# Triangular inverses in a gated-delta-net layer: two row groups' 32x32 products issued alternately, and the third set of products issued at once

## The chip, the cores and the metric

The kernel runs on one core of one Trainium2 chip. The time is that of one execution on the device, in microseconds (us), of the slowest core, which here is the only one. Matrix products run on TensorE (PE in the profile), the loads of their stationary operands are counted apart (PEld), and the other engines are VectorE (DVE), ScalarE (ACT), GpSimd (POOL) and SyncE (SP), which here only issues DMAs.

## The reference, cut to what matters

Two layers on x of 1024 tokens by 1024 features in float32: layer 0 is chunked softmax attention, layer 1 is gated DeltaNet, and each is followed by a dense squared-ReLU MLP. The change lies in layer 1, in the triangular solve of each of its 8 heads:

```python
L = jnp.where(strict, jnp.einsum('bhnid,bhnjd->bhnij', kb, k) * decay, 0.0)
M = L + jnp.eye(CHUNK, dtype=jnp.float32)
rhs = jnp.concatenate([vb, kb * jnp.exp(gc)[..., None]], axis=-1)
sol = lax.linalg.triangular_solve(M, rhs, left_side=True, lower=True, unit_diagonal=True)
u, w = sol[..., :dv], sol[..., dv:]
```

What follows is a scan over the chunks of a head, which multiplies the solution by the state that the chunks before have left.

## The kernel before, in words

Dense products are made of three matmuls each: weights and activations are split into a high and a low part (`whi`, `wlo`, `xs`), and the three larger of the four products are added up in a PSUM bank of 128x512. These are the rows `acc<-xs,whi` and `acc<-xs,wlo` of the profile, and also `zz<-xs,...` at first.

The DeltaNet layer (`deltanet`, L1700, `dn_run`, L1844) runs 34 panels of dense products (k, q, v and z of 8 heads, and the first two of the output projection), 24 matmuls for each half of a panel. After each single dense matmul it calls `turn` (L1753): every side task that is due gets to issue one step, up to its next `yield`. The side tasks are generators: the blocks of L (`dn_blocks`), the inverses (`dn_inverses`, L2379), the preparation of keys, queries and values, two interleaved scans (`dn_scans`, L2488) and the heads' outputs (`dn_outs`). So the order of the instructions on every engine is fixed when the program is written out. What decides it is a planner's clock (`Clock`, L91), with a price for each instruction: a dense matmul counts 512/2400 us, and a float32 product 32 columns wide counts 32/600 us. A task that has issued a step is due again when the planner takes that step for finished (`t.ready = c.end`), 0.3 us after its last matmul if it ended on TensorE. A task can also wait for another's mark (`until`), for a buffer (`take`) or for a planned time (`sleep`). On the chip each engine then takes its own instructions in that order, held up by semaphores alone. All instructions that are issued under the planner carry the line of its wrapper, L162, so that in the profile they are told apart by tiles.

The kernel takes chunks of 128 tokens, 8 for each head, and inverts each 128x128 triangle by blocks. The four 32x32 blocks on the diagonal are inverted on VectorE in `dn_solves` (L2221), for four heads together; through DRAM they come into `Z` (the tile `Zh`) and, transposed, into `X`. `dn_inverse` (L2290), once for each head, puts in the rest:

- Step 1 (L2319 to L2327): for the two 64x64 triangles of a chunk (e = 0 and 1), the block beside the diagonal (`U12`, tile `ua`) times `X`. These are 8 products of 32x32 (one for each chunk p) for each e. A product with e = 0 reads partitions 0 to 31 and writes 32 to 63; one with e = 1 reads 64 to 95 and writes 96 to 127. In the profile they are `tp<-X,ua`. VectorE then scales both results into `ua` (L2330, `ua<-tp,nbr`).
- Step 2 (L2333 to L2340): these times the inverted diagonal blocks of `Z`, again 8 products for each e, here reading partitions 32 to 63 or 96 to 127 (`tp<-Zh,ua`).
- After a `yield`, 8 further products for e = 0 alone with the operands exchanged (L2341 to L2343, `tp<-ua,Zh`), into the same PSUM tile `tp`; I call these the third group. After another `yield` ScalarE copies all of it out (L2345 to L2348, `X<-tp` and `Zh<-tp`).
- Two further steps of 64x64 products (`tp<-X,ub` and `tp<-Zh,ub`) complete the inverse.

A float32 product stands in the trace as two passes, each a weight load and a matmul, so 16 products are 32 rows of the trace. All products of a step go into one PSUM bank (`tp`, taken in turn from two). Before the change the 8 products with e = 0 come first and then the 8 with e = 1.

Of the kernel before, what the change touches and what calls it, by code (L numbers as in the profile page):

```python
# [39 lines left out]
def wide(col, p, n):  # L40

    return col.rearrange("p (q o) -> p q o", o=1).broadcast_to([p, col.shape[-1], n])
# [191 lines left out]
class Trunk:  # L234
# [2055 lines left out]
    def dn_inverse(self, h):  # L2290

        nc, db = self.nc, self.db
        Z = self.Zh[h % 3]
        X = self.X[:, :, 0:32]
        U12 = self.dq.tile([P, 8, 32], F32, name=self.nm("ua"), tag="ua")
        U34 = self.dq.tile([P, 8, 64], F32, name=self.nm("ub"), tag="ub")
        for e in range(2):
            nc.sync.dma_start(U12[64 * e : 64 * e + 32], self.u12[h, e])
        nc.sync.dma_start(U34[0:64], self.u34[h])
        nbr = self.sm.tile([P, 8], F32, name=self.nm("nbr"), tag="nbr")  # L2300
        nc.vector.scalar_tensor_tensor(nbr, self.rk[:, h], -1.0, self.cols[:, 1, h], ALU.mult, ALU.mult)
        yield from self.sleep(G["sl_u12"])
        for e in range(2):
            r = slice(64 * e, 64 * e + 32)
            nc.gpsimd.tensor_tensor(U12[r], U12[r], wide(self.rk[r, h], 32, 32), ALU.mult)
        nc.gpsimd.tensor_tensor(U34[0:64], U34[0:64], wide(self.rk[0:64, h], 64, 64), ALU.mult)
        yield from self.until("solve", h // 4)
        if h >= 3:
            yield from self.until("scan", h - 3)
        zd, xd = self.solved[h // 4]  # L2310
        for b in range(4):
            r = slice(b * 32 + (h % 4) * 8, b * 32 + (h % 4) * 8 + 8)
            s = slice(32 * b, 32 * b + 32)
            nc.sync.dma_start(Z[s, :, s], zd[r].rearrange("p c i -> c p i"))
            if b < 3:
                nc.sync.dma_start(self.X[s, :, 32 * (b % 2) : 32 * (b % 2) + 32], xd[r].rearrange("p c i -> c p i"))
        yield from self.sleep(G["sl_inv"] if h % 4 == 0 else G["sl_inv2"])
        yield
        tp = yield from self.take("tp")  # L2319
        ps = tp[:, :256].rearrange("p (q t) -> p q t", t=32)  # L2320
        hT = U12
        for e in range(2):
            r, o = slice(64 * e, 64 * e + 32), slice(64 * e + 32, 64 * e + 64)
            for p in range(8):
                nc.tensor.matmul(ps[o, p], U12[r, p], X[r, p], start=True, stop=True,
                                 tile_position=(64 * e, 64 * e + 32))
        yield  # L2327
        for e in range(2):
            o = slice(64 * e + 32, 64 * e + 64)
            nc.vector.tensor_tensor(hT[o], ps[o], wide(nbr[o], 32, 32), ALU.mult)  # L2330
        self.give("tp", tp)
        yield
        tp = yield from self.take("tp")  # L2333
        ps = tp[:, :256].rearrange("p (q t) -> p q t", t=32)
        for e in range(2):
            r, o = slice(64 * e, 64 * e + 32), slice(64 * e + 32, 64 * e + 64)
            for p in range(8):
                nc.tensor.matmul(ps[r, p], hT[o, p], Z[o, p, o], start=True, stop=True,
                                 tile_position=(64 * e + 32, 64 * e))
        yield  # L2340
        o = slice(32, 64)  # L2341
        for p in range(8):
            nc.tensor.matmul(ps[o, p], Z[o, p, o], hT[o, p], start=True, stop=True, tile_position=(32, 32))  # L2343
        yield
        nc.scalar.activation(self.X[o, :, 0:32], ps[o], AF.Copy)  # L2345
        for e in range(2):
            r, o = slice(64 * e, 64 * e + 32), slice(64 * e + 32, 64 * e + 64)
            nc.scalar.activation(Z[r, :, o], ps[r], AF.Copy)  # L2348
        self.give("tp", tp)
        yield  # L2350
        tp = yield from self.take("tp")
        ps = tp.rearrange("p (q t) -> p q t", t=64)
        r, o = slice(0, 64), slice(64, 128)
        for p in range(8):
            nc.tensor.matmul(ps[o, p], U34[r, p], self.X[r, p], start=True, stop=True, tile_position=(0, 64))
        yield
        nc.vector.tensor_tensor(U34[o], ps[o], wide(nbr[o], 64, 64), ALU.mult)
        self.give("tp", tp)
        yield
        tp = yield from self.take("tp")  # L2360
        ps = tp.rearrange("p (q t) -> p q t", t=64)
        for p in range(8):
            nc.tensor.matmul(ps[r, p], U34[o, p], Z[o, p, o], start=True, stop=True, tile_position=(64, 0))
        yield
        nc.scalar.activation(Z[r, :, o], ps[r], AF.Copy)
        self.give("tp", tp)
        yield
# [351 lines left out]
```

## Time and profile before

| | |
|---|---|
| median of the runs | 2487.07 us |
| the three runs | 2490.65, 2485.62, 2487.07 us |
| time of the profiled execution | 2484.63 us |
| its span, first to last instruction | 2482.9 us |
| mean granted TensorE clock | 0.995 |
| DVE, ACT, POOL busy, share of the span | 72%, 47%, 50% |
| the inverses' steps lie between | 1390 and 1635 us of the span |

The span leaves out 1.7 us of the profiled execution. Busy time of matmuls counts from a row's start to its modelled end, so the rows of a pipelined sequence overlap; how fast such a sequence runs is read from the starts of its rows.

### The profile page before, as it was taken

What the parts mean: (1) busy time and instruction counts of PE and PEld (TensorE: products, weight loads), DVE (VectorE), ACT (ScalarE), POOL (GpSimd) and SP (SyncE); (2) the same over time, 40 slices, a digit from 0 to 9 for tenths busy, and PEclk for the clock granted to TensorE, in tenths of its full rate; (3) what the DMA queues carried; (4) which work ended last, traced back from release to release, by engine and by line L of the source; (5) the groups of instructions that cost most, each with busy time, mean ns of one, the idle gap of its engine ahead of it and who ended that gap; (6) DMA issues with size and microseconds to landing.
All of it is one profiled execution on the core that took longest, in us unless ns stands there. A gap on an engine that the chain in (4) does not pass through costs nothing.

```text
span 2482.9 us, 36204 instructions
## 1 busy us (share of the span) xinstructions
PE 2417.5 (97%) x12556; PEld 2014.5 (81%) x12556; DVE 1789.9 (72%) x3152; ACT 1168.9 (47%) x2209; POOL 1250.5 (50%) x1059
## 2 busy tenths in 40 slices
PE   8999999999999999999999999999999999999997
PEld 6888888777788887887787888888787888888886
DVE  6666656678877678888778776665678777688887
ACT  6666666635455433333463443343345555433333
POOL 2444445623766656666444443433316666476655
PEclk9999999999999999999999999999999999999998
DMA  4222232522555796763265322322415555967842
GB/s 163 70 67 67 73 84 91 185 88 102 216 212 208 277 335 215 255 211 116 97 194 180 93 85 90 92 75 81 182 60 201 201 216 214 354 233 238 257 163 85
DMA packets 199927, 398.92 MB, mean 161 GB/s; under 512 B 53232, under 2 KB 67888, under 8 KB 199744
## 3 DMA queue, kind: packets, MB, share of 16 engines
q1 hardware_dynamic: 180016, 351.50, 42.3%
q10 hardware_dynamic: 19728, 45.12, 4.8%
q8 instruction: 99, 1.62, 0.3%
q14 instruction: 84, 0.69, 0.1%
HBM read 257.43 MB, written 130.71 MB: 156 GB/s over the span
## 4 chain that ended last, share of the span: by engine, by line
PE 70%; DVE 6%; DMA 2%; issue 1%; ACT 1%; POOL 0%; ACTq 0%; DVEq 0%; POOLq 0%; SPq 0%
PE y L1039 26%; PE z L1039 12%; PE acc L162 12%; PE acc L1039 7%; PE tp L162 4%; PE zz L162 2%; PE acc L303 2%; PE acc L305 2%; PE acc L304 2%; PE sb L162 2%; DVE x L1544 1%; DMA wraw<-in_w_up_dram 1%; DVE xs L420 0%; DMA xd<-x 0%; DMA qk<-grows 0%
## 5 line engine op out<-in xcount | busy, mean ns | idle before, releaser
L162 PE MATMUL acc<-xs,whi 128*128 128x512 f32 x1728 | 597.6, 409 | 4.1 <-POOL whi L1043 1.0
L162 PEld LDWEIGHTS acc<-xs,whi 128*128 128x128 f32 x1728 | 315.8, 189 | 53.0 <-POOL whi L1043 1.4
L162 PE MATMUL acc<-xs,wlo 128*128 128x512 f32 x856 | 348.4, 407 | 0.0
L1039 PE MATMUL y<-xs,whi 128*128 128x512 f32 x1008 | 311.6, 390 | 5.2 <-DVE x L1544 1.8
L162 POOL TENSOR_TENSOR wlo<-wraw,whi 128x512 fp32r<-128x512 f32 x126 | 165.4, 1314 | 224.2 <-ACT whi L162 190.6
L1054 POOL TENSOR_TENSOR s<-wraw 128x256 f32<-128x256 f32 (+1 forms) x93 | 90.1, 969 | 358.6 <-DVE a L1045 172.1
L1045 DVE TENSOR_TENSOR wlo<-wraw,whi 128x512 fp32r<-128x512 f32 (+1 forms) x182 | 209.4, 1151 | 25.6 <-ACT whi L1048 25.6
L1039 PEld LDWEIGHTS y<-xs,whi 128*128 128x128 f32 x1008 | 188.9, 188 | 47.1 <-DVE x L1544 2.6
L1048 ACT ACTIVATE whi<-wraw 128x512 fp32r<-128x512 f32 (+2 forms) x191 | 146.4, 766 | 121.7 <-PE y L1039 83.0
L1048 ACT ACTIVATE a<-s 128x256 fp32r<-128x256 f32 x122 | 63.8, 524 | 281.7 <-PE y L1039 141.3
L1039 PE MATMUL y<-xs,wlo 128*128 128x512 f32 x504 | 196.4, 390 | 0.0
L1039 PE MATMUL y<-xs,a 128*128 128x512 f32 x732 | 187.9, 392 | 6.5 <-DVE x L1544 6.5
L1544 DVE TENSOR_TENSOR x<-y,x 128x512 f32<-128x512 f32 x240 | 165.0, 687 | 35.1 <-PE y L1039 28.3
L162 PEld LDWEIGHTS acc<-xs,wlo 128*128 128x128 f32 x856 | 162.4, 190 | 23.2
L1039 PEld LDWEIGHTS y<-xs,a 128*128 128x128 f32 x732 | 136.1, 188 | 40.1 <-DVE x L1544 10.3
L1039 PE MATMUL y<-xs,ahi 128*128 128x512 f32 x512 | 158.9, 391 | 7.8 <-ACT nt L1233 7.8
L1039 PE MATMUL acc<-xs,whi 128*128 128x512 f32 x528 | 162.9, 390 | 0.0
L162 POOL TENSOR_SCALAR pr<-pr,rs 128x640 f32<-128x640 f32 (+4 forms) x128 | 88.6, 696 | 129.0 <-DVE rs L162 99.9
L1039 PE MATMUL z<-xs,whi 128*128 128x512 f32 x480 | 147.8, 389 | 0.0
L1121 DVE TENSOR_TENSOR c<-c 128x512 fp32r<-128x512 f32 x112 | 119.9, 1077 | 30.8 <-POOL c L1051 27.3
L162 DVE CUSTOM_DVE_ANT_0 pr<-sp,bias 128x640 f32<-128x640 f32 (+4 forms) x128 | 83.8, 655 | 63.9 <-PE sp L162 62.9
L162 POOL TENSOR_TENSOR cy<-cy,cz 128x512 f32<-128x512 f32 x48 | 62.7, 1306 | 126.9 <-DVE cz L162 95.8
(370 smaller groups left out, 6047.8 us busy)
## 6 DMA issues: line engine op xcount, KB each, us to landing
xs<-gt SPq DMA_DIRECT2D x256, 256.0 KB, 4.9
gt<-c SPq DMA_DIRECT2D x112, 512.0 KB, 3.0
wraw<-in_w_up_dram SPq DMA_DIRECT2D x64, 512.0 KB, 3.7
wraw<-in_w_down_dram SPq DMA_DIRECT2D x64, 512.0 KB, 4.6
r<-gr SPq DMA_DIRECT2D x88, 256.0 KB, 3.5
wraw<-in_w_in_dram SPq DMA_DIRECT2D x32, 512.0 KB, 3.5
gr<-ssum ACTq DMA_DIRECT2D x62, 256.0 KB, 3.2
wraw<-in_w_qkv_dram SPq DMA_DIRECT2D x30, 512.0 KB, 3.3
```

The lines of the kernel that those rows point to most:

```text
L162: return call(*args, **more)
L303: nc.tensor.matmul(ps, hi[:, k], xh, start=(k == 0), stop=False)
L304: nc.tensor.matmul(ps, hi[:, k], xl, start=False, stop=False)
L305: nc.tensor.matmul(ps, lo[:, k], xh, start=False, stop=(k == KT - 1))
L1039: nc.tensor.matmul(ps, w[:, k], x, start=bool(first and f), stop=bool(last and e), skip_group_check=True)
L1045: self.nc.vector.tensor_tensor(lo, src, hi.bitcast(F32), ALU.subtract)
L1048: self.nc.scalar.activation(hi, src, AF.Copy)
L1054: self.nc.gpsimd.tensor_tensor(out, x, y, ALU.add)
L1121: nc.vector.tensor_tensor(t[z][:, HB:].bitcast(F32R), t[z][:, HB:], t[z][:, :HB], ALU.subtract)
L1544: nc.vector.tensor_tensor(x, ps, x, ALU.add)
```

## The change

In steps 1 and 2 the two loops are exchanged: for each chunk p the product with e = 0 and then that with e = 1 are issued, so that the two row groups alternate one by one. The `yield` between step 2 and the third group is taken out, so that the third group's 8 products follow at once, in the same turn of the planner. Number, operands and places of the products stay.

```diff
-        for e in range(2):
-            r, o = slice(64 * e, 64 * e + 32), slice(64 * e + 32, 64 * e + 64)
-            for p in range(8):
+        for p in range(8):
+            for e in range(2):
+                r, o = slice(64 * e, 64 * e + 32), slice(64 * e + 32, 64 * e + 64)
                 nc.tensor.matmul(ps[o, p], U12[r, p], X[r, p], start=True, stop=True,
                                  tile_position=(64 * e, 64 * e + 32))
         yield
...
-        for e in range(2):
-            r, o = slice(64 * e, 64 * e + 32), slice(64 * e + 32, 64 * e + 64)
-            for p in range(8):
+        for p in range(8):
+            for e in range(2):
+                r, o = slice(64 * e, 64 * e + 32), slice(64 * e + 32, 64 * e + 64)
                 nc.tensor.matmul(ps[r, p], hT[o, p], Z[o, p, o], start=True, stop=True,
                                  tile_position=(64 * e + 32, 64 * e))
-        yield
         o = slice(32, 64)
         for p in range(8):
             nc.tensor.matmul(ps[o, p], Z[o, p, o], hT[o, p], start=True, stop=True, tile_position=(32, 32))
```

## The prediction

> **What bounds the kernel now.** I read the page first, then busy times by stretch, then TensorE's waits around the inverses.
>
> ```profile
> span 2482.9 us, 36204 instructions
> PE 2417.5 (97%) x12556; PEld 2014.5 (81%) x12556; DVE 1789.9 (72%) x3152; ACT 1168.9 (47%) x2209; POOL 1250.5 (50%) x1059
> ```
>
> The busy times by stretch (columns: PE, PEld, DVE, ACT, POOL, the granted clock, DMA):
>
> ```profile
> 1340.00:1640.00 300.00, 298.51 (x2346) 252.94 (x2345) 208.53 (x497) 118.88 (x272) 119.46 (x94) 1.00 0.30 90
> 1640.00:1740.00 100.00, 100.00 (x574) 85.30 (x573) 53.32 (x131) 38.31 (x89) 35.44 (x26) 1.00 0.27 85
> 1740.00:1760.00 20.00, 15.37 (x64) 11.27 (x64) 14.35 (x26) 8.79 (x18) 10.24 (x7) 0.91 0.67 232
> ```
>
> TensorE is busy 298.51 of the 300 us that hold the inverses, and all of the next 100. DVE, the next busiest, has 91 us free in the first stretch. The waits of TensorE between 1385 and 1760 us say the same from the other side:
>
> ```profile
> PE tp L162 <- DVE o L162: 2.9, 1, 2.9
> PE tp L162 <- POOL dc L162: 1.3, 1, 1.3
> PE acc L162 <- ACT xs L162: 0.8, 1, 0.8
> PE sb L162 <- ACT vn L162: 0.4, 1, 0.4
> ```
>
> One wait of 1.3 us belongs to the inverses' stretch; most of the rest is the stage's end. So in this stage a microsecond less on TensorE is nearly a microsecond less of time, unless the new order makes an instruction wait where none did. Whether the inverses are themselves waited for is read from the products that use them:
>
> ```profile
> L162 PE MATMUL zz<-vb,Zh x12: 270/272/275, 1465.0 to 1713.5; 128*128 128x128 f32 x12
> L162 PE MATMUL sb<-vb,Zh x4: 272/274/275, 1405.1 to 1488.9; 128*128 128x128 f32 x4
> L162 ACT ACTIVATE Zh<-tp x24: 373/375/593, 1396.2 to 1634.1; 32x256 f32<-32x256 f32 x16, 64x512 f32<-64x512 f32 x8
> ```
>
> A head's scan begins with its `vb,Zh` product. The last inverse is copied out at 1634.1 us, and the last scan begins 79 us later. An earlier inverse alone therefore brings little. What counts is time on TensorE.
>
> **What step 1 and step 2 cost now.** The matmuls of head 0 from step 1's end to the third group, then one step of head 0, both steps of head 1 and step 2 of head 7 (start, length from the first start to the last end, count):
>
> ```profile
> 1391.87 0.62 PE L162 MATMUL acc<-xs,whi 128*128 128x512 f32 x2
> 1392.33 0.40 PE L162 MATMUL acc<-xs,wlo 128*128 128x512 f32 x1
> 1392.57 0.62 PE L162 MATMUL acc<-xs,whi 128*128 128x512 f32 x2
> 1393.03 0.40 PE L162 MATMUL acc<-xs,wlo 128*128 128x512 f32 x1
> 1393.35 1.09 PE L162 MATMUL tp<-Zh,ua 32*32 32x32 f32 x32
> 1394.38 0.74 PE L162 MATMUL acc<-xs,whi 128*128 128x512 f32 x2
> 1395.05 0.69 PE L162 MATMUL tp<-ua,Zh 32*32 32x32 f32 x16
> 1395.67 0.50 PE L162 MATMUL acc<-xs,wlo 128*128 128x512 f32 x1
> ...
> 1390.35 1.25 PE L162 MATMUL tp<-X,ua 32*32 32x32 f32 x32
> ...
> 1412.47 1.09 PE L162 MATMUL tp<-X,ua 32*32 32x32 f32 x32
> ...
> 1415.53 1.09 PE L162 MATMUL tp<-Zh,ua 32*32 32x32 f32 x32
> 1416.55 0.66 PE L162 MATMUL tp<-ident,qT 128*128 128x128 f32 x4
> ...
> 1418.51 0.69 PE L162 MATMUL tp<-ua,Zh 32*32 32x32 f32 x16
> ...
> 1625.79 1.09 PE L162 MATMUL tp<-Zh,ua 32*32 32x32 f32 x32
> ```
>
> ```profile
> L162 PE MATMUL tp<-Zh,ua x256: 191/191/212, 1393.4 to 1626.7; 32*32 32x32 f32 x128
> ```
>
> One pass lasts 0.19 us, but they are pipelined: 16 passes of one row group take 0.69 us, so 0.50 from the first start to the last, 0.50/15 = 0.033 us apart. Two groups one after the other would take 0.69 + 16 x 0.032 = 1.20 us. They take 1.09. The missing 0.11 lies where the one group gives way to the other, as a count of the passes in step 2 of head 0 shows. Each row begins at 1393.35, and the number in brackets is how many passes have started by its end:
>
> ```profile
> 1393.35:1393.65 0.30, 0.30 (x9) 1.00 1.14 135
> 1393.35:1393.75 0.40, 0.40 (x12) 1.00 1.00 135
> 1393.35:1393.85 0.50, 0.50 (x18) 1.00 0.93 134
> 1393.35:1393.95 0.60, 0.60 (x22) 1.00 0.92 139
> 1393.35:1394.05 0.70, 0.70 (x25) 1.00 0.97 148
> 1393.35:1394.15 0.80, 0.80 (x28) 1.00 0.92 145
> ```
>
> Three passes start in a tenth of a microsecond everywhere, but six between .75 and .85. There the second group already runs while the first's last passes do: TensorE works on both row groups at a time, each at its own pace. It does so only for the few passes that it looks ahead.
>
> **What alternation takes away.** If neighbours in the order always belong to different groups, that overlap holds throughout, and 32 passes take the 0.69 us of one group plus the second's later start. That start is between 0 and one product (two passes, 0.06 us) behind; I take 0.02, hence 0.71 us. The saving is 1.09 - 0.71 = 0.38 us a step. The bounds are 0.40 (no lag) and -0.11 (none of even today's overlap). Of the 16 steps I take 15: head 0's first step takes 1.25 us today, without visible overlap, and the rows do not say what its second group waited for, so I put its saving at zero. 15 x 0.38 = **5.7 us**.
>
> The Trainium skill speaks against this in "TensorE: Matmul & The Clock Gate" (Wait — 56ns, not 53.3ns?): start-to-start never drops below about 25 ns however few the columns are. By that figure a step of 32 passes would come to about 0.97 us by my estimate, and this term to 1.8 us. The trace disagrees at one place, where six starts in 0.1 us are 17 ns apart; no row here shows it for a whole step.
>
> **What the missing `yield` takes away.** Around a step of small products TensorE loses time. Dense matmuls start 0.23 us apart (three from 1392.33 to 1393.03). From step 2's last start (1393.35 + 1.09 - 0.19 = 1394.25) to the third group's first (1395.05) pass 0.80 us with only two dense matmuls in them. Those two cost 0.46 elsewhere, and one step from pass to pass is 0.03, so 0.31 us is paid for leaving the small products and coming back. With the third group directly behind step 2 this is paid once less in each head, whatever stood between (two dense matmuls in head 0, transposes and scan products among others in head 1): 8 x 0.31 = **2.5 us**. From below I bound this by 0, if the two groups' tile positions make the same break; from above by 0.31 + 0.11, if the third group also overlaps the end of step 2's second row group as the groups do now.
>
> **What moves.** The third group issues 8 matmuls and no DMA. It passes what the planner had put between: 2.1 us of work in head 1 (from 1415.53 + 0.90 to 1418.51), 0.8 in head 0. That work starts about 0.5 us later, scan products and transposes among it, and the ACT copies behind the third group come earlier. Behind a late scan product stand a DVE step and the next products of that scan, and their cover is the dense matmuls between; without it a scan step would cost up to its 0.5 us, at most 8 x 0.5 = 4 us. In the alternating order the second product of a step needs the second group's operands, which came 8 products later before. An operand that is late holds the step up no longer than now, since the step's end waited for it anyway. But all 16 products, and the dense ones behind, then stand in line. For step 2 these operands are DVE's scaled results:
>
> ```profile
> 1391.64 0.88 DVE L162 TENSOR_TENSOR ua<-tp,nbr 32x256 f32<-32x256 f32 x2 [0.80 <-PE tp L162]
> ```
>
> In head 0 both are done at 1392.52, 0.83 us before step 2 begins. I cost both effects at nothing and keep the 4 us for the range. From the first head on, the planner may also place later steps of all tasks otherwise, on every queue, SP's and POOL's included. The trace cannot show that, and it is the largest unknown.
>
> **The sum.** 5.7 + 2.5 = 8.2 us off the profiled execution's 2484.63 us gives 2476.4. That execution lay 2.4 us below the median of the three runs; off the median, 2487.07, it gives **2478.9 us**, or 2479.
>
> **The rivals.**
>
> *The overlap does not hold for a whole step.* Both groups write one PSUM bank, and one meeting of three or four passes is all the trace shows. A pace limit midway between the two that the rows show (17 and 33 ns, so 25) would leave a step at 31 x 0.025 + 0.19 = 0.97 us, so 15 x 0.12 + 2.5 = 4.3 us in all: 2482.8. With passes strictly one after the other (1.20 us), the steps lose 15 x 0.11 = 1.7 us, and 2487.07 - 2.5 + 1.7 = 2486.3 is left. For it: the passes at the meeting may have been queued beforehand. Against it: six starts in 0.1 us is exactly double the pace, with both groups in one bank. The Trainium skill states the rule for the strict case in "TensorEngine Tiling (Array Packing)" (Gotcha 1: PSUM Pressure): different row tiles cannot use the same PSUM bank at the same time. By that rule the trace would have no such meeting, and it has one.
>
> *Changing the row group costs something each time.* This is the rival on the slower side. Today each step changes the group once, afterwards 15 times: 14 x 2 x 8 = 224 changes more. At the price of entering a group of small products from dense ones (1393.03 to 1393.35 is 0.32 us, less 0.23, so 0.09), that is 20.2 us, and with today's overlap lost too the time is 2487.07 - 2.5 + 1.7 + 20.2 = 2506.5. It is slower than before from (2.5 - 1.7)/224 = 0.004 us a change. Against it: the one change that a step has now costs less than nothing.
>
> *The gain is eaten by new waits.* TensorE gets ahead, and the chain through the last head's normalization, which it awaits 2.9 us at the stage's end, or that through POOL (1.3 us) does not follow. If half is lost, 2483; if all, 2487. With another idle stretch like the last one, whose window has a clock of 0.91, so 0.09 x 20 = 1.8 us, it is 2489. For it: the order of all later work may shift. Against it: the scans interleave with dense matmuls, and TensorE's four longest waits of the stage add up to 5.4 us. The same shift can gain, too: without these waits and the slow clock (2.9 + 1.3 + 1.8 = 6.0) the time is 2473.
>
> **How the numbers follow.** About 0.2% (5 us) is what a measurement of this kernel can tell from no change, so faster means below 2482.1. I give the forecast 0.60, the incomplete overlap 0.15 (0.09 for the pace limit, 0.06 for strict order), a price per change 0.04 and the eaten gain 0.21. Of the forecast's cases some 0.05 end above 2482.1 by small new waits; of the eaten gain 0.03 stay below. That makes faster 0.58. Slower takes the 0.04 and some 0.05 of the eaten gain whose waits exceed what was won by 5 us: 0.09. The rest, 0.33, is no change. The range goes from 2473, with the stage's own waits gone as well, to 2489, which takes in the incomplete overlap and most of the eaten gain.
>
> **What would show it.** In the changed profile the 32-pass rows, or the count of starts, tell the first term: about 0.7 us a step and six starts in 0.1 us throughout if right; 0.97 or 1.2 if a rival holds. The third group must follow step 2 with no dense matmul between, 48 passes in one stretch of about 1.2 us, and 8 entries less. TensorE's waits between 1385 and 1760 us must stay near these 5.4 us. I am wrong if the steps shrink as said and the time does not: then the waits have grown, and the one that did is named there.

## The result

The changed kernel takes 2478.56 us in the median (2475.62 to 2479.61, 7 runs), the kernel before, timed beside it, 2485.62 us (2481.44 to 2490.65, 7 runs). The ratio is 0.9971 with a 95% interval of 0.9961 to 0.9981: faster by 0.19 to 0.39%, or about 7 us. A second timing on another occasion (below, the last experiment) gave 0.9974 (0.9963 to 0.9984). The forecast was 2479.

The profiled execution after took 2476.15 us. Its page begins:

```profile
span 2474.4 us, 36203 instructions
PE 2406.7 (97%) x12556; PEld 2006.3 (81%) x12556; DVE 1785.7 (72%) x3152; ACT 1169.3 (47%) x2209; POOL 1248.1 (50%) x1059
```

TensorE has as many matmuls as before and is busy 10.8 us less. The span is 8.5 us shorter, but not all of that is the change. The first step 1 began at 1390.35 us before. After, it begins here:

```profile
1387.51 0.24 PE L162 MATMUL tp<-X,ua 32*32 32x32 f32 x2
1388.01 0.69 PE L162 MATMUL tp<-X,ua 32*32 32x32 f32 x30 [0.25 <-DMA X<-xd]
...
1750.71 0.39 PE L303 MATMUL acc<-xs,whi 128*128 128x512 f32 x1
```

Up to that point both programs issue the same instructions in the same order, so 2.84 us of the difference is variation between two executions. (The changed kernel, profiled once more in the last experiment, began this step at 1391.19 us.) What the change does lies behind it. The second row names what head 0's first step waits for here, the landing of `X`, 0.25 us. The last row quoted is the first matmul outside the planned stage. In the profile before, that matmul is

```profile
1759.33 0.39 PE L303 MATMUL acc<-xs,whi 128*128 128x512 f32 x1
```

From the first step 1 to there, the stage took 1759.33 - 1390.35 = 368.98 us before and 1750.71 - 1387.51 = 363.20 us after: 5.8 us less. I use this stage length below, since it leaves out what varied ahead of the change.

**The steps.** Head 1 after (the rows of both steps and the third group; start, length, count):

```profile
1410.19 0.69 PE L162 MATMUL tp<-X,ua 32*32 32x32 f32 x32
...
1412.86 0.60 PE L162 MATMUL tp<-Zh,ua 32*32 32x32 f32 x26
1413.27 0.21 PE L162 MATMUL tp<-ua,Zh 32*32 32x32 f32 x1
...
1413.39 0.57 PE L162 MATMUL tp<-ua,Zh 32*32 32x32 f32 x13
1413.89 0.66 PE L162 MATMUL tp<-ident,qT 128*128 128x128 f32 x4
```

Step 1 takes 0.69 us, as long as one row group alone. How many of its passes have started by the end of each window (the number in brackets):

```profile
1410.18:1410.28 0.10, 0.09 (x6) 1.00 0.02 0
1410.18:1410.48 0.30, 0.29 (x18) 1.00 0.01 0
1410.18:1410.68 0.50, 0.49 (x30) 1.00 0.01 0
```

Six start in each tenth of a microsecond, from the first pass to the last. Step 2 and the third group are one stretch of 48 passes without a dense matmul, 1.10 us from 1412.86 to 1413.39 + 0.57. The third group's first pass starts while six passes of step 2 are still to come.

**The waits.** TensorE's between 1385 and 1755 us after:

```profile
PE tp L162 <- DVE o L162: 2.8, 1, 2.8
PE tp L162 <- DVE vb L162: 1.6, 1, 1.6
PE tp L162 <- DVE kd L162: 1.4, 1, 1.4
PE zz L162 <- DVE st L162: 1.0, 1, 1.0
PE acc L162 <- ACT xs L162: 0.8, 1, 0.8
```

The wait for POOL of 1.3 us is gone, and three waits for DVE of 1.0 to 1.6 us, 4.0 in all, have come. With the smaller rows the list adds up to 8.9 us against 6.0 before.

**The clock.** The windows at the stage's end, before, after, and in a second profile of the changed kernel (the number behind POOL's is the granted clock):

```profile
1725.00:1759.33 34.33, 29.70 (x146) 23.48 (x145) 23.43 (x48) 14.71 (x32) 13.62 (x10) 0.95 0.52 174
```

```profile
1716.00:1750.71 34.71, 30.23 (x149) 23.98 (x148) 23.45 (x49) 14.70 (x32) 13.95 (x10) 0.90 0.51 172
```

```profile
1720.03:1754.74 34.71, 30.08 (x149) 23.89 (x148) 23.56 (x49) 14.70 (x32) 14.03 (x10) 0.95 0.52 172
```

In the first profile after, the clock withheld 0.10 x 34.7 = 3.5 us instead of 0.05 x 34.3 = 1.7. That is a difference between executions and not the change's doing: the second profile of the same kernel has 0.95 like the kernel before. Nor did it lengthen the stage, which takes 363.55 us in the second profile and 363.20 in the first.

### The profile page after: what moved, and what is told of

It is laid out like the page before. It is cut to its first block, busy times and chain, and to the rows that moved or that the text cites. A ratio compares the mean times of both kernels' runs of the same rounds, so it can differ in the third digit from the quotient of the medians.

```text
span 2474.4 us, 36203 instructions
## 1 busy us (share of the span) xinstructions
PE 2406.7 (97%) x12556; PEld 2006.3 (81%) x12556; DVE 1785.7 (72%) x3152; ACT 1169.3 (47%) x2209; POOL 1248.1 (50%) x1059
## 4 chain that ended last, share of the span: by engine, by line
PE 70%; DVE 5%; DMA 2%; issue 1%; ACT 1%; POOL 0%; SPq 0%; ACTq 0%; DVEq 0%; POOLq 0%
PE y L1039 27%; PE z L1039 13%; PE acc L162 11%; PE acc L1039 7%; PE tp L162 3%; PE zz L162 2%; PE acc L303 2%; PE acc L305 2%; PE acc L304 2%; PE sb L162 1%; DVE x L1544 1%; DMA wraw<-in_w_in_dram 1%; DMA wraw<-in_w_up_dram 1%; DVE xs L420 0%; DMA xd<-x 0%
```

## The experiments

The theory: the gain is time on TensorE, from both parts, less what the planner's new order loses. The first rival: the new order itself made the gain, and TensorE's own time mattered little. It can be told apart, because exchanging the loops leaves the planner's prices and with them the order of everything else as it was; only the missing `yield` changes that order. The traces bear this out: apart from the inverses' own products, TensorE, VectorE, ScalarE and GpSimd go through the same sequence of instructions in the kernel before and with the loops alone exchanged, and again in the changed kernel and with the `yield` alone taken out. In each experiment the ratio is to the kernel before, run on the same chip. The stage lengths, read as above in each trace, stand in a table at the end.

### Alternation alone

```diff
 (before, with the loops over p and e exchanged in steps 1 and 2)
                 nc.tensor.matmul(ps[r, p], hT[o, p], Z[o, p, o], start=True, stop=True,
                                  tile_position=(64 * e + 32, 64 * e))
         yield
```

> The row groups alternate in steps 1 and 2, the yield before the third group stays; every engine's order but that of the 32x32 products is the one of before. If the gain is TensorE time: steps of 32 passes in 0.69 us instead of 1.09, 15 x 0.40 = 6.0 us less, ratio to before about 0.9976, and the long waits of TensorE are those of before (2.9, 1.3, 0.8 us). Rival, that the planner's new order made the gain: ratio 1.000, since this order is the old one.

Measured: 2478.01 us, ratio 0.9975 (0.9965 to 0.9985). Head 1, and the wait that the changed kernel no longer has:

```profile
1411.67 0.69 PE L162 MATMUL tp<-X,ua 32*32 32x32 f32 x32
1414.33 0.69 PE L162 MATMUL tp<-Zh,ua 32*32 32x32 f32 x32
...
1416.91 0.69 PE L162 MATMUL tp<-ua,Zh 32*32 32x32 f32 x16
```

```profile
PE tp L162 <- POOL dc L162: 1.3, 1, 1.3
```

In the old order the alternation alone gives 0.25%, as expected from the steps. The rival is refuted: with the order unchanged there should have been nothing. The stage is 4.8 us shorter where the steps give 6.0. Of the rest, 0.8 us are longer waits (6.8 us in all against 6.0), most of it in one place, behind this row of DVE:

```profile
1598.25 2.27 DVE L162 TENSOR_SCALAR ry<-rt 128x8 int32<-128x8 int32 x1
...
1600.83 0.49 PE L162 MATMUL zz<-r,Zh 128*128 128x128 f32 x2 [0.64 <-DVE r L162]
```

In the kernel before the same `ry<-rt` takes 2.28 us, and TensorE, which reaches this point later, does not wait. What makes the row so long is the subject of the experiment with VectorE.

### The third group at once, alone

```diff
 (before)
                 nc.tensor.matmul(ps[r, p], hT[o, p], Z[o, p, o], start=True, stop=True,
                                  tile_position=(64 * e + 32, 64 * e))
-        yield
         o = slice(32, 64)
```

> The old loops (first all products of one row group, then of the other), but the third group follows at once; the order of all other instructions is that of the changed kernel. If the gain is TensorE time: 0.31 us of leaving and coming back and 0.10 of overlap at the third group's start, 8 x 0.41 = 3.3 us less, and the new order's longer waits give back about 2.7 us: ratio 0.9986 to 1.000. Rival, that the new order made the gain: ratio 0.997 as for the whole change.

Measured: 2481.91 us, ratio 0.9991 (0.9982 to 0.9999). Step 2 and the third group of head 1, and the waits:

```profile
1416.04 1.00 PE L162 MATMUL tp<-Zh,ua 32*32 32x32 f32 x29
...
1416.97 0.57 PE L162 MATMUL tp<-ua,Zh 32*32 32x32 f32 x13
```

```profile
PE tp L162 <- DVE vb L162: 1.6, 1, 1.6
PE tp L162 <- DVE kd L162: 1.0, 1, 1.0
PE zz L162 <- DVE st L162: 1.0, 1, 1.0
```

The 48 passes take 1.50 us (1416.04 to 1416.97 + 0.57), 0.10 less than 1.09 and 16 further passes 0.032 us apart. So the third group overlaps the end of step 2 here too. The three new waits are here, with the old loops: they come from the order. They give back most of what this part wins (the waits add up to 8.4 us against 6.0); it is worth about 0.1% by itself, and the stage is only 0.3 us shorter. The first rival asked for 0.997 here and is refuted a second time. On top of alternation the missing `yield` shortens the stage by 0.6 to 1.0 us (364.15 against 363.55 and 363.20), which the times do not resolve: 0.9975 against 0.9974 and 0.9971.

### Row groups changing after every four products

```diff
 (before, in both steps)
-        for e in range(2):
+        for b in range(4):
+            e = b % 2
             r, o = slice(64 * e, 64 * e + 32), slice(64 * e + 32, 64 * e + 64)
-            for p in range(8):
+            for p in range(4 * (b // 2), 4 * (b // 2) + 4):
```

> As before, yield kept, but the row groups change after every four products (e = 0, 1, 0, 1) instead of after eight: three meetings in a step instead of one. If TensorE looks only some three passes ahead, each meeting wins 0.10 us: 32 passes in 1.20 - 0.30 = 0.90 us (first start to last end). Rival, that it overlaps whatever stands in its queue: 0.7 us, as when they alternate one by one. Rival, that a meeting's overlap needs the queue filled beforehand: 1.09 us as before.

Measured in a single execution (2480.44 us, too few to compare times):

```profile
1409.89 0.89 PE L162 MATMUL tp<-X,ua 32*32 32x32 f32 x32
1412.75 0.89 PE L162 MATMUL tp<-Zh,ua 32*32 32x32 f32 x32
```

0.89 us, where 0.90 was expected from three meetings at 0.10 each. So TensorE does not overlap all 32 passes of a step, although they stand in line together. The rows fit a reach of about three passes (0.10 us at 0.032 a pass) at each meeting; that TensorE looks so far ahead is inferred from these lengths. It is why alternation one by one matters. The stage, 367.45 us, is 1.5 us shorter than before and not the 15 x 0.20 = 3.0 that the steps give. Matched instruction by instruction with the kernel before, it is 1.9 us ahead up to 1545 us of that kernel's span and loses 1.1 in the next 4 us, where the clock fell in this execution and not in that one.

### Three groups alternating

```diff
 (the changed kernel: step 2)
+        c = slice(32, 64)
         for p in range(8):
             for e in range(2):
...
                 nc.tensor.matmul(ps[r, p], hT[o, p], Z[o, p, o], start=True, stop=True,
                                  tile_position=(64 * e + 32, 64 * e))
+            nc.tensor.matmul(ps[c, p], Z[c, p, c], hT[c, p], start=True, stop=True, tile_position=(32, 32))
...
-        for p in range(8):
-            nc.tensor.matmul(ps[o, p], Z[o, p, o], hT[o, p], start=True, stop=True, tile_position=(32, 32))
```

> As the changed kernel, but the third group's products alternate with the two row groups of step 2 one by one (24 products in turn). The third group reads the partitions 32 to 63 like the first row group and writes other columns. If only different row groups overlap, the 32 passes that share a row group run one after the other: about 1.2 us for the 48 passes (first start to last end), 0.1 more than the 1.1 of the changed kernel, and 0.8 us slower than it in all: ratio to before about 0.9975. Rival, that different columns of the same rows overlap too: 48 passes in about 0.7 us, 8 x 0.4 = 3.2 us faster than the changed kernel, ratio about 0.9958.

Measured: 2474.05 us, ratio 0.9961 (0.9947 to 0.9974). Starts of all 48 passes, both kinds together:

```profile
1413.77:1413.97 0.20, 0.19 (x18) 1.00 0.00 0
1413.77:1414.17 0.40, 0.39 (x36) 1.00 0.00 0
1413.77:1414.29 0.52, 0.51 (x48) 1.00 0.00 0
```

All 48 start within 0.52 us, nine in a tenth of a microsecond. My expectation here was wrong and the rival right: products that read the same 32 partitions overlap as well if they write different columns. The stretch shrinks from 1.10 to 0.71 us (0.52 and the last pass), 8 x 0.39 = 3.1 us, and the stage by 3.3.

### The GpSimd products moved to VectorE

```diff
 (three groups alternating, in dn_prep_queries)
-            nc.gpsimd.tensor_tensor(WQ[:, :, 1], ..., ALU.mult)
+            ops = (WQ[:, :, 1], ..., ALU.mult)
+            self.clock.spend("gpsimd", "tensor_tensor", ops, {})
+            nc.vector.real.tensor_tensor(*ops)
```

> As the kernel with three alternating groups, but the 8 products WQ<-qT,row of 128x1024 (2.4 us each on GpSimd) run on VectorE in the same place of the order; the planner's prices stay, so every engine's order is otherwise the same. If VectorE instructions are held up while GpSimd runs such a product, the VectorE rows of 2.3 us on 128x8 operands (ry<-rt, ru<-ru) shrink to about 0.17 us, and of TensorE's waits for DVE kd (1.4), DVE st (1.0) and DVE vb (1.6 us) about 2 to 3 us go, against 1.2 us more of work on VectorE in each head: ratio to before about 0.995. Rival, that these VectorE instructions are long for another reason: the rows of 2.3 us stay, and the ratio is that of three alternating groups, 0.996, or above.

This looks for the cause of the three new waits. In the changed kernel the DVE chain behind the wait for `kd` has this row, and POOL this one beside it:

```profile
1511.92 2.29 DVE L162 TENSOR_SCALAR ry<-rt 128x8 int32<-128x8 int32 x1
1514.12 0.68 DVE L162 TENSOR_TENSOR kd<-tp,ck 128x512 f32<-128x512 f32 x1
```

```profile
1511.81 2.36 POOL L162 TENSOR_TENSOR WQ<-qT,row 128x1024 f32<-128x1024 f32 x1
```

The same instruction elsewhere, in the changed kernel (shortest, median and longest in ns):

```profile
L162 DVE TENSOR_SCALAR ry<-rt x12: 170/172/2289, 1206.7 to 1739.3; 128x8 int32<-128x8 int32 x8, 128x32 int32<-128x32 int32 x2, 128x4 int32<-128x4 int32 x2
```

An operation of 0.17 us lasts 2.29, and ends as POOL's product does (1511.81 + 2.36 = 1514.17). Behind the waits for `vb` and `st` stand VectorE rows of the same kind: `fu<-fu,ry` of 3.84 us and `ru<-ru` of 2.31, each beside one of these products. The old order has such a row as well: the `ry<-rt` shown with alternation alone, 2.27 us from 1598.25, lies beside a product of 2.36 us from 1598.14. So the new order did not bring in the long rows. It decides which VectorE operations meet a product, and the faster steps decide whether TensorE comes early enough to wait behind one. With these products on VectorE:

```profile
L162 DVE TENSOR_SCALAR ry<-rt x12: 170/172/1218, 1206.9 to 1733.2; 128x8 int32<-128x8 int32 x8, 128x32 int32<-128x32 int32 x2, 128x4 int32<-128x4 int32 x2
```

```profile
PE tp L162 <- DVE o L162: 2.4, 1, 2.4
PE acc L162 <- ACT xs L162: 0.9, 1, 0.9
PE sb L162 <- ACT vn L162: 0.4, 1, 0.4
```

Measured: 2471.48 us, ratio 0.9953 (0.994 to 0.9965), and a stage 3.5 us shorter than with three groups alone. The two ratios, 0.9953 and 0.9961, are too close to tell apart; the reading rests on the waits and the stage. All three new waits (1.6, 1.4 and 1.0 us) are gone, with every order otherwise kept. The longest such row is 1.22 us, not the 0.17 I expected: GpSimd has other products, and they stayed; this row lies beside a `wlo` of 1.30 us. So the products of one engine lengthen rows of another; ahead of the prediction I wrote that semaphores alone hold an engine up. The Trainium skill, "SBUF — State Buffer" (Who interferes with whom), says that VectorE and GpSimd share one pair of SBUF ports under a lock, and that some VectorE instructions wait until a GpSimd instruction is done. The rows agree.

### 64x64 products in two column groups

```diff
 (three groups alternating; the first of the last two steps, the second likewise)
         for p in range(8):
-            nc.tensor.matmul(ps[o, p], U34[r, p], self.X[r, p], start=True, stop=True, tile_position=(0, 64))
+            d = (o, r)[p % 2]
+            nc.tensor.matmul(ps[d, p], U34[r, p], self.X[r, p], start=True, stop=True, tile_position=(0, d.start))
...
+        for n, d in enumerate((o, r)):
+            nc.vector.real.tensor_tensor(U34[o, n::2], ps[d, n::2], wide(nbr[o, n::2], 64, 64), ALU.mult)
```

> As the kernel with three alternating groups, and in the two steps of 64x64 products every second chunk's product writes the other 64 columns, so that neighbours lie in different column groups of the same rows; the copies out of PSUM are split in two (even and odd chunks). Orders otherwise the same. If different columns of the same rows overlap as in three alternating groups, a step's 16 passes take about 0.7 us instead of 1.14, 16 x 0.45 = 7.2 us less: ratio to before about 0.993. Rival, that this held for 32x32 tiles alone: 1.14 us as now, ratio 0.996.

Measured: 2469.16 us, ratio 0.9946 (0.9932 to 0.9959). The two steps of head 0 in the changed kernel, then here:

```profile
1393.73 1.14 PE L162 MATMUL tp<-X,ub 64*64 64x64 f32 x16
1396.83 1.14 PE L162 MATMUL tp<-Zh,ub 64*64 64x64 f32 x16
```

```profile
1394.23 0.68 PE L162 MATMUL tp<-X,ub 64*64 64x64 f32 x16
1396.88 0.68 PE L162 MATMUL tp<-Zh,ub 64*64 64x64 f32 x16
```

The steps shrink by 0.46 us as expected, 16 x 0.46 = 7.4 us, but the stage by only 3.8, and the ratio, 0.9946 after 0.9961, by about half of what was expected. TensorE's waits grew little (the list adds up to 8.9 us, 8.7 with three groups alone). The clock did more. Two windows with three groups alone, and then here:

```profile
1500.00:1530.00 30.00, 28.60 (x266) 24.54 (x265) 21.15 (x50) 12.21 (x30) 10.38 (x8) 1.00 0.39 108
1725.00:1755.00 30.00, 25.63 (x114) 19.73 (x114) 18.35 (x32) 12.06 (x25) 12.84 (x9) 0.89 0.63 233
```

```profile
1500.00:1530.00 30.00, 28.60 (x261) 23.97 (x260) 22.05 (x51) 14.26 (x33) 13.28 (x11) 0.94 0.40 113
1725.00:1755.00 30.00, 26.07 (x100) 19.78 (x100) 17.09 (x27) 13.26 (x25) 12.41 (x9) 0.83 0.72 256
```

0.06 of 30 us twice is 3.6 us of withheld clock, and 3.6 us are missing. Not all of it is lost time, though. Matched instruction by instruction, the two profiles show 1.5 us lost where the first window's clock fell and 1.1 at the stage's end; 0.5 more go to the wait for `st`, 1.4 us instead of 1.0. What brought the lower clock no experiment here shows.

### Both together

```diff
 (64x64 products in two column groups, and WQ<-qT,row on VectorE)
```

> The two kernels before in one: WQ products on VectorE and 64x64 products in two column groups. If both effects are time on TensorE's path, they add up: ratio to before about 0.992 (0.9961 less 0.0029 less 0.001). Rival, that TensorE gets so far ahead that VectorE's added work is waited for: ratio 0.993 or above, with new waits on DVE.

Measured: 2462.63 us, ratio 0.9916 (0.9902 to 0.9929). The waits are those of the chain through the last head and little else:

```profile
PE tp L162 <- DVE o L162: 2.9, 1, 2.9
PE acc L162 <- ACT xs L162: 0.8, 1, 0.8
```

The effects add up, a little better than by the sum: against the products on VectorE alone, the stage is 7.5 us shorter, all that the two column groups save in the steps. This is the fastest version: it beats both kernels, and lies about 0.6% below the changed one timed on the same chip (2462.63 against 2477.95 us).

### The changed kernel once more

> The changed kernel on the same chip as these, to set beside them: ratio to before 0.997; steps of 0.69 us, waits of TensorE for DVE vb, kd and st of 1.6, 1.4 and 1.0 us again, since they come from the order and not from chance.

Measured: 2477.95 us, ratio 0.9974 (0.9963 to 0.9984), with the waits for `vb`, `kd` and `st` at 1.7, 1.4 and 1.0 us. The new waits are a property of the order.

| kernel | stage length, us | against before | ratio of the times |
|---|---|---|---|
| before | 368.98 | | |
| changed | 363.20 | -5.8 | 0.9971 |
| changed, once more | 363.55 | -5.4 | 0.9974 |
| alternation alone | 364.15 | -4.8 | 0.9975 |
| changing after four products | 367.45 | -1.5 | one execution |
| at once alone | 368.69 | -0.3 | 0.9991 |
| three groups alternating | 359.91 | -9.1 | 0.9961 |
| and WQ on VectorE | 356.38 | -12.6 | 0.9953 |
| and 64x64 in two column groups | 356.15 | -12.8 | 0.9946 |
| all of these | 348.87 | -20.1 | 0.9916 |

The row with WQ on VectorE and the one with 64x64 products each add to three groups alternating. Every stage length is that of one execution and holds what the clock withheld in it, so differences of a microsecond between rows settle nothing by themselves.

## Why the prediction was right

- **The bound.** TensorE's time is what counts in this stage. Alternation alone, in an unchanged order, took 15 x 0.40 = 6.0 us off the steps, and 4.8 off the stage.
- **The overlap of the row groups.** It was read from one meeting of a few passes. It holds for whole steps, with a lag of almost nothing: 0.69 us instead of my 0.71, so 6.0 instead of 5.7 us. Head 0's first step, which I left out, took 1.18 us in one profile of the changed kernel and 1.36 in the other, against 1.25.
- **Leaving and coming back.** The term of 0.31 us a head was sized too low. The third group also overlaps the end of step 2 by 0.10, which I had as the upper bound (1.10 us for the 48 passes, not 1.2): 8 x 0.41 = 3.3 instead of 2.5 us. No row shows the 0.31 by itself. It fits the difference to alternation alone, where the stage is 0.6 to 1.0 us longer with 2.1 to 2.4 us less of waits, 3.0 in all.
- **What moves.** This is the step of the prediction that failed in size: I cost the new order at nothing. It brought 2.9 us more of waits (8.9 against 6.0): 4.0 of new ones, less the 1.3 for POOL that went, and 0.2 of small ones. The new ones stand behind DVE rows that GpSimd's products held up, and go when one kind of these products leaves GpSimd. Nor is the order alone to blame: with the order unchanged, the faster steps already made TensorE wait 0.64 us behind such a row. My own sign of being wrong, waits that leave the 5.4 us, was there; the steps' larger saving hid it in the time.
- **The sum.** 6.0 + 3.3 = 9.3 us of steps, less 2.9 of waits, is 6.4. The stage shows 5.8. In the second profile, with 3.2 of waits, it is 5.4 where the sum gives 6.1. What took the remaining 0.6 to 0.7 stays open. So two terms were a little too small, and the loss left out was larger than what they lacked. Of the 2.5 us that I gave the missing `yield`, it brought 0.3 to 1.0, once its waits are paid. That the median of 2478.56 us meets the forecast of 2478.9 so closely is luck: I took 8.2 us off 2487.07, the median of three runs, while the seven runs give 7.1 us off 2485.62, and the two errors cancel. The profiled pair's 8.5 owes 2.84 us to what happened ahead of the first step.
- **The rivals.** A pace limit of 25 ns is refuted: with two groups six passes start in 0.1 us throughout, with three groups nine. So is the one of a shared PSUM bank, since all these passes write one. A price for each change of the row group does not exist here: the time per pass halves. The gain eaten by new waits was the right rival, though not through the two chains that it named: TensorE waits for the last head's `o` as long as before (2.8 and 2.9 us), and the wait for POOL went. It took less than a third of the 9.3 us.

## What to carry to other kernels

Where small products use a corner of TensorE's array (32*32 of 128*128 here), put products of different tile positions next to each other in the order, one by one: blocks of eight, of four and single products took 1.09, 0.89 and 0.69 us for the same 32 passes. It need not be another row group; other columns of the same rows serve as well, so a product whose place in PSUM is free can be put into other columns. And when a planner fixes the order, measure a change of the order apart from a change of the work: here they had opposite signs, and the loss had its cause on two engines that the change did not touch.

## What the runs showed of the hardware that was not expected

Products of 32x32 in the same rows and different columns ran together: 48 passes on three tile positions started within 0.52 us, 11 ns apart, where one position alone starts a pass every 32 ns. The Trainium skill, "TensorE: Matmul & The Clock Gate" (Part 3: Packing small matmuls, The mechanism), says that weight loads overlap matmuls in flight only when the row group differs. The three-group rows and the 64x64 rows (1.14 to 0.68 us with the same rows) disagree for this kernel: in both, passes of one row group kept double the pace once their columns differed. A VectorE operation on 128x8 numbers of 0.17 us lasted 2.29 us beside a GpSimd product of 2.36.
